# Recurrence of a two-layer hybrid block: adaLN loads asked for three places ahead, their products handed out at two points of a step

## The chip, the cores and the metric

One core of a Trainium2 chip. The metric is device time of one execution in microseconds. Times are in us unless marked otherwise. Engines: PE (matmuls; PEld is its weight load), DVE, ACT, POOL, and SP, which here only issues DMAs.

## The reference, cut to what matters

Two layers over 512 latent and 256 context tokens, width 1024. Each layer mixes with a gated linear recurrence (eight heads of 64, two directions) beside differential attention, then an MLP. Everything is modulated by six vectors of 1024 that one small product per layer makes from the conditioning vectors (adaLN):

```python
mod  = (sc  @ ada_w[l] + ada_b[l])[:, None, :]     # ada_w[l]: 1024 x 6144, fp32
modc =  scc @ ada_w[l] + ada_b[l]
sh1, s1, g1, sh2, s2, g2 = jnp.split(mod, 6, axis=-1)
...
def step(state, inp):                               # the recurrence, per token
    sa = jnp.einsum("bhvk,bhk->bhv", state, kk_t)
    state = state * w_t - sa * b_t + v_t * k_t
    y = jnp.einsum("bhvk,bhk->bhv", state, r_t)
...
o = jnp.concatenate([o_r, o_d], axis=-1) @ w_out[l]
x = x + g1 * rms_norm(o, g_post_mix[l])
f = sq_relu_mlp(modulate(rms_norm(x, g_pre_mlp[l]), sh2, s2), w_ff1[l], w_ff2[l])
x = x + g2 * rms_norm(f, g_post_mlp[l])
```

## The kernel before

The order of instructions on each engine is set when the program is built, by a scheduler that plays the program against a timeline of its own; each engine then runs its list strictly in order and waits at the head of it. Python code fixes the priorities: what is traced first goes first where both are ready.

A layer has three phases. `phase_wr` streams w_in, makes the recurrence's inputs and the attention, and ends with the recurrence (`rest`). `phase_o` multiplies by w_out, `phase_f` is the MLP. All weights come through one ring of three SBUF places of 512 KB (`raw`, tags raw0 to raw2), issued by SP: the w_in pieces, then the ada_w pieces of the recurrence, then the w_out pieces. A place is free again when the product or the split that reads it is done.

The recurrence has 12 steps a layer: six chunks of 128 tokens (`n`), two halves each (`j`), and in each step both directions (`d`) in turn. `step` yields behind each part: X of d = 0 and of d = 1 (PE lines 1186 and 1189, then ACT makes `xs` from it), `us` (L1198) and its copy `uv`, the state update (`us` again, L1210, then DVE's `sc` and ACT's `sbd`), and the output (L1226). That is eight yields; the last step has six (no state update), and in layer 2 the first four steps have six (no output). At each yield other work is handed out: `prep_b` of later chunks (L977 to L1054), the triangular inverses (`inv`, DVE lines 1100 and 1102, with relays through DRAM: `da`, `N`, `W`, `dn`, `dt`, `TT`, S<-dn; `merge` is L1152 to L1162 on PE) and the finish of completed token tiles (L1281 to L1295).

The adaLN product of the later vectors is such filler too. `ada_half` makes 512 columns of one vector from four pieces of ada_w; each piece is one `raw` load and eight small matmuls into `adar` (L265). Layer 1 needs 48 pieces (its own three kinds and the next layer's first), layer 2 needs 32. `ada` is a queue with credits: each step gives `ADA[l]` = 4 of them, all at the first yield, and the loads of that block are traced behind the step's own `uv` load on SP:

```python
for _ in step(n, j):
    work(1)
    if nst == 0:
        with tc.issue_after(self.gate.ins):
            ada(ADA[l])
    nst += 1
```

A product's load is traced just ahead of the product. `issue_after(x)` lets what a block traces on x's engine stand only behind x in that engine's list. In layer 1 the queue runs to the end of the last step; in layer 2 it is empty after the ninth.

Of the kernel before, what the change touches and what calls it, by code (L numbers as in the profile page):

```python
# [26 lines left out]
ADA = [4, 4]  # L27
# [137 lines left out]
class K:  # L165
# [16 lines left out]
    def run(self):  # L182
        with ExitStack() as es:
            self.cp = self.pool(es, "const", 1)
            self.sm = self.pool(es, "small", 6)
            self.rp = self.pool(es, "rowp", 1)
            self.rawp, self.raws, self.rawn = self.pool(es, "rawp", 1), 3, 0
            self.dr = es.enter_context(self.tc.tile_pool(name="dr", bufs=1, space=DRAM))
            self.setup()
            for l in range(L):  # L190
                self.layer(l)
                if self.stop is not None and self.stop.startswith(f"{l}"):
                    return
# [63 lines left out]
    def ada_half(self, l, ch, hf, ps, tag):  # L257

        nc = self.nc
        acc = ps.tile([128, 128], F32, name=self.n("adar"), tag=tag, bufs=1 if tag == "a" else 2)  # L260
        for kp in range(4):
            raw = self.raw(self.I["ada_w"][l, ch, hf, kp // 2][:, 2 * (kp % 2):2 * (kp % 2) + 2], [128, 2, 512])
            for k in range(2):
                for g in range(4):
                    nc.tensor.matmul(acc[32 * g:32 * g + 32, :], self.sc[:, 2 * kp + k, :],  # L265
                                     raw[:, k, g * 128:g * 128 + 128], start=(kp + k == 0), stop=(kp == 3 and k == 1),
                                     skip_group_check=True)
            if kp < 3:
                yield
        self.acc = acc  # L270

    def ada_cols(self, l, kind, ps, tag="m"):
# [653 lines left out]
    def recurrence(self, l, last, es, side):  # L926
# [240 lines left out]
        def step(n, j):  # L1167
            need_y = not (last and n < 2)
            final = n == 5 and j == 1
            mw = 128 if need_y else 64  # L1170
# [9 lines left out]
            for d in range(2):  # L1180
# [7 lines left out]
                for p in range(4):  # L1188
                    nc.tensor.matmul(X[0:mw, p * 128:p * 128 + 128], s["KR"][:, 2 * p + q, 0:mw], sbd[:, d, p, :],  # L1189
                                     start=False, stop=False, skip_group_check=True)  # L1190
# [3 lines left out]
            for d in range(2):  # L1194
                s = S[d]
                up = us[:, d]
                for h in range(8):
                    nc.tensor.matmul(up[(h % 2) * 64:(h % 2) * 64 + 64, h // 2, :], s["G"][:, h - h % 2 + s["q"], h % 2, 0:64],  # L1198
                                     s["xs"][:, h * 64:h * 64 + 64], start=True, stop=True, skip_group_check=True)
                for hf in range(2):  # L1200
                    nc.scalar.copy(s["uv"][0:64, hf:8:2, :], up[hf * 64:hf * 64 + 64])
                yield
            if not final:
                for d in range(2):
# [3 lines left out]
                    for h in range(8):  # L1208
                        hs = slice((h % 2) * 64, (h % 2) * 64 + 64)
                        nc.tensor.matmul(sp[hs, h // 2, :], s["BN"][:, h - h % 2 + q, hs], s["uv"][:, h, :],  # L1210
                                         start=True, stop=True, skip_group_check=True)
# [92 lines left out]
        def rest():  # L1304
# [16 lines left out]
            if l == 0:  # L1321
                ada.add(self.ada_cols(1, "mix", pa, "a"))
            work = Fill()
            prep_until(1)
            invs = Fill()
            for n in range(6):
# [3 lines left out]
                for j in range(2):  # L1330
                    nst = 0
                    for _ in step(n, j):
                        work(1)
                        if nst == 0:
                            with tc.issue_after(self.gate.ins):
                                ada(ADA[l])
                        nst += 1

                        for _ in range(4):
# [400 lines left out]
```

## Time and profile before

| | us |
|---|---|
| median of 3 runs | 2432.26 |
| the runs | 2419.16, 2433.48, 2432.26 |
| the profiled execution | 2426.55 |
| its span | 2424.8 |
| recurrence of layer 1, in the span | 490 to 757 |
| recurrence of layer 2 | 1756 to 2004 |

The span runs from the first to the last instruction; 1.75 us lie around it. The two recurrences are found by the products L1186 to L1226, which stand nowhere else. PEclk is the share of the full TensorE clock that was granted; 0.50 is 1.2 GHz and 1.00 is 2.4 GHz.

### The profile page before, as it was taken

What the parts mean: (1) busy time and instruction counts of PE and PEld (TensorE: products, weight loads), DVE (VectorE), ACT (ScalarE), POOL (GpSimd) and SP (SyncE); (2) the same over time, 40 slices, a digit from 0 to 9 for tenths busy, and PEclk for the clock granted to TensorE, in tenths of its full rate; (3) what the DMA queues carried; (4) which work ended last, traced back from release to release, by engine and by line L of the source; (5) the groups of instructions that cost most, each with busy time, mean ns of one, the idle gap of its engine ahead of it and who ended that gap; (6) DMA issues with size and microseconds to landing.
All of it is one profiled execution on the core that took longest, in us unless ns stands there. A gap on an engine that the chain in (4) does not pass through costs nothing.

```text
span 2424.8 us, 43738 instructions
## 1 busy us (share of the span) xinstructions
PE 2250.5 (93%) x17150; PEld 1903.9 (79%) x17150; DVE 1518.5 (63%) x2629; ACT 1174.4 (48%) x2393; POOL 803.6 (33%) x1048
## 2 busy tenths in 40 slices
PE   6999998899988999999999999999879988999997
PEld 5887887787777988888888887778767877788886
DVE  5456458647755675555556736665856575778784
ACT  4345547545534544333344435555735544555552
POOL 1212324832212343333330422323562121553530
PEclk9999999779998999999999999999879988999999
DMA  7543445377577521111112344454567664423230
GB/s 275 157 131 87 122 126 134 81 207 186 148 190 221 196 92 60 64 61 62 61 63 85 136 137 133 115 144 110 115 171 198 153 181 161 165 88 121 86 114 35
DMA packets 291630, 313.67 MB, mean 129 GB/s; under 512 B 139680, under 2 KB 220896, under 8 KB 291424
## 3 DMA queue, kind: packets, MB, share of 16 engines
q1 hardware_dynamic: 280320, 284.66, 38.8%
q0 software_dynamic: 10240, 23.08, 5.0%
q8 instruction: 135, 2.21, 0.4%
q10 hardware_dynamic: 864, 3.15, 0.3%
q14 instruction: 71, 0.58, 0.1%
HBM read 257.04 MB, written 53.77 MB: 128 GB/s over the span
## 4 chain that ended last, share of the span: by engine, by line
PE 66%; DVE 10%; DMA 8%; issue 5%; POOL 4%; ACT 4%; SPq 2%; ACTq 0%; POOLq 0%; DVEq 0%
PE pf L351 32%; PE pu L351 16%; PE po L351 4%; DMA raw<-in_ada_w 2%; PE po L832 2%; PE pb L1046 2%; PE sc L795 1%; DVE wl L1500 1%; POOL pr L1100 1%; POOL W L1102 1%; PE X L1189 1%; DVE nm L797 1%; PE X L1226 1%; PE adar L265 1%; PE ptr L815 1%
## 5 line engine op out<-in xcount | busy, mean ns | idle before, releaser
L1500 DVE TENSOR_TENSOR wl<-raw,wh 128x1024 fp32r<-128x1024 f32 x170 | 255.8, 1507 | 125.0 <-ACT wh L1499 124.2
L351 PE MATMUL pf<-hl,wh 128*128 128x512 f32 (+1 forms) x832 | 282.1, 342 | 0.0
L351 PE MATMUL pf<-hh,wh 128*128 128x512 f32 (+1 forms) x832 | 280.5, 342 | 0.6 <-ACT hh L397 0.6
L351 PE MATMUL pf<-hh,wl 128*128 128x512 f32 (+1 forms) x832 | 275.7, 342 | 0.0
L1499 ACT ACTIVATE wh<-raw 128x1024 fp32r<-128x1024 f32 x170 | 179.2, 1058 | 161.5 <-PE pf L351 143.9
L351 PE MATMUL pf<-wh,fah 128*128 128x512 f32 x570 | 224.5, 396 | 13.2 <-DVE fu L1633 7.2
L351 PE MATMUL pu<-hh,wh 128*128 128x512 f32 (+1 forms) x632 | 223.7, 354 | 4.8 <-DVE t L557 1.7
L351 PE MATMUL pf<-wl,fah 128*128 128x512 f32 x570 | 223.9, 394 | 0.7 <-DVE wl L1500 0.7
L351 PE MATMUL pf<-wh,fal 128*128 128x512 f32 x570 | 221.4, 394 | 1.8 <-DVE fal L1600 1.8
L351 PE MATMUL pu<-hh,wl 128*128 128x512 f32 (+1 forms) x632 | 218.6, 346 | 4.0 <-DVE wl L340 4.0
L351 PE MATMUL pu<-hl,wh 128*128 128x512 f32 (+1 forms) x632 | 218.0, 345 | 0.0
L797 DVE TENSOR_REDUCE nm<-sc 128x1 f32<-128x768 f32 (+1 forms) x160 | 132.5, 841 | 79.3 <-PE sc L795 78.5
L351 PEld LDWEIGHTS pf<-hl,wh 128*128 128x128 f32 x832 | 156.6, 188 | 20.0 <-DVE hl L399 0.2
L351 PEld LDWEIGHTS pf<-hh,wl 128*128 128x128 f32 x832 | 156.1, 188 | 20.0
L351 PEld LDWEIGHTS pf<-hh,wh 128*128 128x128 f32 x832 | 155.3, 188 | 20.4 <-ACT hh L397 0.8
L799 ACT ACTIVATE e<-sc,nm 128x768 f32<-128x768 f32 (+1 forms) x160 | 130.7, 821 | 53.9 <-DVE nm L797 44.3
L321 POOL TENSOR_TENSOR rs<-ms,pw 128x1 f32<-128x1 f32 (+2 forms) x60 | 56.7, 948 | 271.2 <-DVE ms L319 270.5
L351 PEld LDWEIGHTS pu<-hh,wh 128*128 128x128 f32 x632 | 121.2, 192 | 23.4 <-DVE t L557 2.4
L351 PEld LDWEIGHTS pf<-wh,fah 128*128 128x128 f32 x570 | 107.2, 188 | 40.6 <-ACT fah L1599 13.6
L1633 DVE TENSOR_TENSOR acc<-pf,acc 128x512 f32<-128x512 f32 x155 | 104.2, 682 | 53.9 <-PE pf L351 53.3
L351 PEld LDWEIGHTS pu<-hh,wl 128*128 128x128 f32 x632 | 121.0, 192 | 19.0 <-DVE wl L340 4.8
L351 PEld LDWEIGHTS pu<-hl,wh 128*128 128x128 f32 x632 | 121.1, 192 | 14.3 <-issue 1.7
(262 smaller groups left out, 5607.1 us busy)
## 6 DMA issues: line engine op xcount, KB each, us to landing
raw<-in_w_ff SPq DMA_DIRECT2D x128, 512.0 KB, 3.7
raw<-in_ada_w SPq DMA_DIRECT2D x96, 512.0 KB, 6.5
raw<-in_w_in SPq DMA_DIRECT2D x52, 512.0 KB, 4.0
ld<-zd SPq DMA_DIRECT2D x40, 384.0 KB, 5.5
ks<-qd POOLq DMA_DIRECT2D x64, 192.0 KB, 5.4
zd<-zr SPq DMA_DIRECT2D x22, 384.0 KB
raw<-in_w_out SPq DMA_DIRECT2D x16, 512.0 KB, 5.9
qs<-qd POOLq DMA_DIRECT2D x32, 192.0 KB, 5.9
```

The lines of the kernel that those rows point to most:

```text
L265: nc.tensor.matmul(acc[32 * g:32 * g + 32, :], self.sc[:, 2 * kp + k, :], raw[:, k, g * 128:g * 128 + 128], start=(kp + k == 0), stop=(kp ...
L321: nc.gpsimd.tensor_tensor(r, m, self.pw1.to_broadcast([128, cols]), ALU.pow)
L351: nc.tensor.matmul(out, a, b, start=(start and i == 0 and j == 0), stop=(i == n - 1 and j == 2), skip_group_check=not start)
L795: nc.tensor.matmul(sc[:, k0:k1], qs[:, br, tk], ks[:, br, k0:k1], start=True, stop=True)
L797: nc.vector.tensor_reduce(nm, sc, AX.X, ALU.max, negate=True)
L799: nc.scalar.activation(ee, sc, AF.Exp, bias=nm, accum_out=ls[:, br:br + 1])
L815: nc.tensor.transpose(pt[:, (k - k0) * 128:(k - k0) * 128 + 128], e[0][:, k * 128:k * 128 + 128], self.ident)
L832: nc.tensor.matmul(po, pT[:, k * 128:k * 128 + 128], vn[:, k, h * 64:h * 64 + 64], start=(k == 0), stop=(k == nk - 1))
L1046: nc.tensor.matmul(pgt[:, u, 0:nn], BK[hs, u, :], KR[hs, 2 * pp + u, 0:nn], start=True, stop=True, skip_group_check=True)
L1499: nc.scalar.activation(hi, src, AF.Copy)
L1500: nc.vector.tensor_tensor(lo, src, hi.bitcast(F32), sub)
L1633: nc.vector.tensor_tensor(d, p, d, add)
```

## The change

Loads and products are taken apart. `ada_todo` lists all pieces of a layer in the order of their products. Three loads are traced ahead of the first step, into the three places of the ring; then each product, once traced, asks for the piece three places on. `ada_half` takes the oldest load from `ada_ring`. The products are handed out at two points of a step, two credits each: at the second yield (behind X of d = 1) and at the sixth (behind the state update of d = 1; in steps of six yields the last one). `self.mark` is the last matmul traced by the step, and the block is traced behind it on PE as well as behind the `uv` load on SP.

```diff
+            self.ada_ring, self.ada_todo = [], iter(())
...
         for kp in range(4):
-            raw = self.raw(self.I["ada_w"][l, ch, hf, kp // 2][:, 2 * (kp % 2):2 * (kp % 2) + 2], [128, 2, 512])
+            raw = self.ada_ring.pop(0) if self.ada_ring else self.ada_load(l, ch, hf, kp)
...
+            self.ada_ahead(1)
             if kp < 3:
                 yield
         self.acc = acc
+
+    def ada_load(self, l, ch, hf, kp):
+        return self.raw(self.I["ada_w"][l, ch, hf, kp // 2][:, 2 * (kp % 2):2 * (kp % 2) + 2], [128, 2, 512])
+
+    def ada_ahead(self, n):
+        self.ada_ring.extend(self.ada_load(*p) for p in islice(self.ada_todo, n))
...
-                    nc.tensor.matmul(X[0:mw, p * 128:p * 128 + 128], s["KR"][:, 2 * p + q, 0:mw], sbd[:, d, p, :],
+                    self.mark = nc.tensor.matmul(X[0:mw, p * 128:p * 128 + 128], s["KR"][:, 2 * p + q, 0:mw], sbd[:, d, p, :],
...
+            self.ada_todo = ((m, ch, hf, kp) for m, chs in [(l, (2,)), (l, (3, 4)), (l, (5,))] + [(1, (0, 1))] * (1 - l)
+                             for hf in range(2) for ch in chs for kp in range(4))
+            self.ada_ahead(self.raws)
             work = Fill()
...
                     for _ in step(n, j):
                         work(1)
-                        if nst == 0:
-                            with tc.issue_after(self.gate.ins):
-                                ada(ADA[l])
                         nst += 1
+
+                        if nst in (2, 6):
+                            with tc.issue_after(self.gate.ins), tc.issue_after(self.mark.ins):
+                                ada(ADA[l] // 2)
```

The same `self.mark =` stands before the matmuls of `us` (L1198 of before) and of the state update (L1210). Lines below the first insertion move by one, those below `ada_load` by nine.

PE at the start of the third step of layer 1, before. `us` is the state update of the step ahead, X is this step's, `adar` the filler, `pb` the preparation of a later chunk.

```order
L1210 MATMUL us_5152<-uv_5680,S_3914 64x64 x8
L1186 MATMUL X_6081<-uv_5977,S_4371 128x64
L1186 MATMUL X_6081<-uv_5977,S_4371 64x64
L1189 MATMUL X_5979<-sbd_3609,S_4135 128x128 x4
L1186 MATMUL X_6081<-uv_5977,S_4371 64x64
L265 MATMUL adar_5995<-raw_6016,sc 32x128 x8
L1186 MATMUL X_6081<-uv_5977,S_4371 64x64 x3
L265 MATMUL adar_5995<-raw_6026,sc 32x128 x8
L1186 MATMUL X_6081<-uv_5977,S_4371 64x64 x2
L1046 MATMUL pb_6143<-S_3658,BK_6127 128x128
L1189 MATMUL X_6081<-sbd_3609,S_4371 128x128 x4
L1198 MATMUL us_5152<-xs_5130,S_4135 64x64 x8
```

The same place after:

```order
L1219 MATMUL us_5152<-uv_5686,S_3914 64x64 x8
L266 MATMUL adar_5730<-raw_5627,sc 32x128 x8
L266 MATMUL adar_5730<-raw_5739,sc 32x128 x8
L1198 MATMUL X_5985<-sbd_3609,S_4135 128x128 x4
L1195 MATMUL X_6042<-uv_5983,S_4371 64x64 x7
L1055 MATMUL pb_6127<-S_3658,BK_6111 128x128 x2
L1198 MATMUL X_6042<-sbd_3609,S_4371 128x128 x4
L266 MATMUL adar_6058<-raw_5749,sc 32x128 x8
L266 MATMUL adar_6058<-raw_5853,sc 32x128 x8
L1207 MATMUL us_5152<-xs_5130,S_4135 64x64 x8
```

The products stood between the parts of X; now two pairs stand behind `us` and behind X of d = 1.

PE at the end of layer 1's last step, before; `po` is the first product with w_out.

```order
L1198 MATMUL us_5152<-xs_5130,S_5374 64x64 x8
L1281 MATMUL pb_8675<-S_4371,cst 128x512
L1281 MATMUL pb_8709<-S_4371,cst 128x512
L265 MATMUL adar_8574<-raw_8725,sc 32x128 x8
L1226 MATMUL X_8545<-uv_8541,S_5374 64x64
L1198 MATMUL us_5152<-xs_5131,S_5501 64x64 x8
L1226 MATMUL X_8545<-uv_8541,S_5374 64x64 x7
L351 MATMUL po_8908<-wh_8780,hh_8770 128x256
```

And after:

```order
L266 MATMUL adar_8594<-raw_8517,sc 32x128 x8
L1235 MATMUL X_8551<-uv_8547,S_5331 64x64
L1207 MATMUL us_5152<-xs_5131,S_5482 64x64 x8
L1235 MATMUL X_8551<-uv_8547,S_5331 64x64 x7
L266 MATMUL adar_8594<-raw_8527,sc 32x128 x8
L1235 MATMUL X_8565<-uv_8549,S_5482 64x64 x8
L266 MATMUL adar_8594<-raw_8587,sc 32x128 x8
L266 MATMUL adar_8594<-raw_8603,sc 32x128 x8
L296 MATMUL adat_8737<-cst,row_8735 128x128
L360 MATMUL po_8908<-wh_8780,hh_8770 128x256
```

The last piece stood ahead of the last `us`; now the last three stand behind it. SP at the same place, before:

```order
L254 DMA raw_8595<-in_ada_w 128x1024
L1263 DMA S_4371<-zd_519 128x4x128
L1400 DMA ol_8838<-od_522 128x4x128
L1400 DMA ol_8850<-od_522 128x4x128
L1295 DMA od_522<-S_4371 128x4x128
L1263 DMA S_4371<-zd_519 128x4x128
L1264 DMA S_4371<-zd_519 128x4x128
L1400 DMA ol_8854<-od_522 128x4x128
L1295 DMA od_522<-S_4371 128x4x128
L1263 DMA S_4371<-zd_519 128x4x128
L254 DMA raw_8725<-in_ada_w 128x1024
L254 DMA raw_8826<-in_w_out 128x1024
```

And after:

```order
L255 DMA raw_8517<-in_ada_w 128x1024
L255 DMA raw_8527<-in_ada_w 128x1024
L1414 DMA ol_8858<-od_522 128x4x128
L1414 DMA ol_8862<-od_522 128x4x128
L1414 DMA ol_8874<-od_522 128x4x128
L255 DMA raw_8587<-in_ada_w 128x1024
L1293 DMA S_4371<-gd_520 128x4x128 x2
L255 DMA raw_8603<-in_ada_w 128x1024
L1414 DMA ol_8878<-od_522 128x4x128
L255 DMA raw_8826<-in_w_out 128x1024
```

The first w_out load stands three places behind the load of piece 46 (raw_8527) in the ring, and so behind that piece's product.

## Rows read from the trace of the kernel before

**Rows 1.** The page's chain that ended last, shares of the span by line.

```profile
PE pf L351 32%; PE pu L351 16%; PE po L351 4%; DMA raw<-in_ada_w 2%; PE po L832 2%; PE pb L1046 2%; PE sc L795 1%; DVE wl L1500 1%; POOL pr L1100 1%; POOL W L1102 1%; PE X L1189 1%; DVE nm L797 1%; PE X L1226 1%; PE adar L265 1%; PE ptr L815 1%
```

**Rows 2.** Stretches of the two recurrences: busy us by engine, PEclk, DMA share, GB/s.

```profile
490.00:757.00 267.00, 245.08 (x3463) 197.73 (x3462) 170.11 (x461) 129.22 (x305) 68.12 (x118) 0.87 0.76 197
1756.00:2004.00 248.00, 221.38 (x3206) 183.58 (x3208) 156.03 (x432) 120.46 (x281) 78.11 (x173) 0.86 0.69 178
```

**Rows 3.** PE's waits in 490 to 757: total us, times, longest.

```profile
PE adar L265 <- DMA raw<-in_ada_w: 13.6, 8, 2.8
```

**Rows 4.** PE's waits in 1756 to 2004.

```profile
PE pg L1152 <- DMA TT<-dt: 7.5, 5, 3.4
...
PE adar L265 <- DMA raw<-in_ada_w: 1.0, 2, 0.7
```

**Rows 5.** The chain inside 490 to 757, by line, shares of that stretch.

```profile
by line: DMA raw<-in_ada_w 16.9%; PE pb L1046 11.1%; PE adar L265 8.9%; PE X L1226 8.4%; PE X L1186 7.4%; PE X L1189 7.1%; PE us L1198 4.8%; PE pb L977 4.3%; PE us L1210 3.9%; DMA S<-gd 2.9%; PE pb L1053 2.6%; PE pb L1281 2.5%; DMA ol<-od 2
```

**Rows 6.** PE in 666 to 675.5 and 583 to 598, in order of time.

```profile
666.75 0.69 PE L1210 MATMUL us<-uv,S 128*64 128x64 f32 x16
...
669.90 1.16 PE L1189 MATMUL X<-sbd,S 128*128 128x128 f32 x8
...
674.41 0.65 PE L265 MATMUL adar<-raw,sc 128*32 128x128 f32 x16 [2.73 <-DMA raw<-in_ada_w]
...
583.36 0.69 PE L1210 MATMUL us<-uv,S 128*64 128x64 f32 x16
...
595.31 2.07 PE L1189 MATMUL X<-sbd,S 128*128 128x128 f32 x8
```

**Rows 7.** Loads of line 254 in 490 to 757.

```profile
DMA to landing us min/median/max: 3.7/5.6/8.8
```

**Rows 8.** Stretches at 0.50 of the clock in layer 1's recurrence, columns as in rows 2.

```profile
522.40:536.00 13.60, 13.60 (x214) 11.47 (x213) 2.35 (x6) 3.25 (x7) 0.00 (x0) 0.50 0.85 212
587.30:597.50 10.20, 9.62 (x56) 8.23 (x57) 5.46 (x16) 3.19 (x9) 3.99 (x5) 0.50 0.77 175
611.20:621.40 10.20, 10.20 (x65) 8.00 (x63) 5.42 (x13) 2.10 (x5) 4.02 (x3) 0.50 0.10 17
676.00:679.40 3.40, 3.40 (x45) 2.75 (x45) 1.54 (x7) 1.28 (x3) 0.00 (x0) 0.50 0.67 125
693.10:699.90 6.80, 5.86 (x74) 4.30 (x69) 2.15 (x9) 1.98 (x5) 0.00 (x0) 0.50 0.82 262
727.20:740.80 13.60, 9.78 (x95) 6.74 (x96) 8.34 (x11) 4.74 (x12) 6.04 (x4) 0.50 1.00 296
```

**Rows 9.** The chain in 470 to 810, in order of time: start, us, what.

```profile
565.14 1.09 PE X L1189 x8
...
588.94 2.01 PE X L1189 x8
...
661.90 1.01 PE adar L265 x32
```

**Rows 10.** SP's issues at layer 1's end, in order of time.

```profile
745.92 0.35 SPq L254 DMA_DIRECT2D raw<-in_w_out  x1
...
749.83 0.51 SPq L254 DMA_DIRECT2D raw<-in_w_out  x1
```

**Rows 11.** PE at the same place and where it next waits, in order of time.

```profile
756.23 0.69 PE L1198 MATMUL us<-xs,S 128*64 128x64 f32 x16
...
759.30 0.39 PE L351 MATMUL po<-wl,hh 128*128 128x256 f32 x1
...
787.54 0.38 PE L351 MATMUL po<-wh,hh 128*128 128x256 f32 x1 [1.23 <-ACT hh L1402]
```

**Rows 12.** ACT's split of the second w_out load.

```profile
755.69 1.06 ACT L339 ACTIVATE wh<-raw 128x1024 fp32r<-128x1024 f32 x1 [0.31 <-DMA raw<-in_w_out]
```

**Rows 13.** SP's own waits in 250 to 490, the phase ahead of layer 1's recurrence.

```profile
SPq L254 <- DVE wl L340: 12.4, 2, 11.3
```

**Rows 14.** DMA issues in 490 to 757: KB each, median us to landing.

```profile
N<-da SPq DMA_DIRECT2D x8, 256.0 KB, 8.3
```

More of the change, by code (lines that the diff above doesn't have):

```diff
@@ L1197, in step @@
                 for h in range(8):
-                    nc.tensor.matmul(up[(h % 2) * 64:(h % 2) * 64 + 64, h // 2, :], s["G"][:, h - h % 2 + s["q"], h % 2, 0:64],
+                    self.mark = nc.tensor.matmul(up[(h % 2) * 64:(h % 2) * 64 + 64, h // 2, :], s["G"][:, h - h % 2 + s["q"], h % 2, 0:64],
                                      s["xs"][:, h * 64:h * 64 + 64], start=True, stop=True, skip_group_check=True)
@@ L1209, in step @@
                         hs = slice((h % 2) * 64, (h % 2) * 64 + 64)
-                        nc.tensor.matmul(sp[hs, h // 2, :], s["BN"][:, h - h % 2 + q, hs], s["uv"][:, h, :],
+                        self.mark = nc.tensor.matmul(sp[hs, h // 2, :], s["BN"][:, h - h % 2 + q, hs], s["uv"][:, h, :],
                                          start=True, stop=True, skip_group_check=True)
```

## The prediction

> **What bounds the kernel now.** I read the page's chain first [rows 1]: two thirds of it are PE's products of the big phases, which the change leaves alone; loads of ada_w hold 2% of the span. So the question is the two recurrences, and I cut them out as stretches [rows 2]: 267 us in layer 1, 248 in layer 2, PE busy in 245.08 and 221.38 of them, DVE in 170 and 156, at a mean clock of 0.87 and 0.86. PE is the busiest engine in both. Then PE's own waits: in layer 1 it stood 13.6 us in front of adaLN products whose load had not landed, in eight waits [rows 3]; in layer 2 only 1.0 us, and there the relays of the inverse cost 7.5 us instead [rows 4]. The chain inside layer 1's recurrence names the same load with 16.9% [rows 5], which is 45 us. The reader is to see why 45 and 13.6 differ: the chain counts a load from its issue, while PE still had other products to do; only what is left when it has none is lost. The 13.6 us are what a load can give back directly, and only in layer 1.
>
> **The change, part by part.** All is set against the profiled execution, 2426.55, which lies 5.7 below the median; the sum is then laid on the median.
>
> *Loads three ahead.* The number of loads, products and bytes stays. A load is now asked for when the product three places on its left is done. With products in pairs at the second and the sixth yield, three loads of four have half a step or a whole one until their product. The fourth (asked behind the first product of the sixth yield, needed by the second product at the next step's second yield) has only the way from `us` of the state update to the end of X. In the trace that way took from 667.44 to 671.06, 3.6 us, at its shortest end, and from 584.05 to 597.38, 13.3, at a long one [rows 6]. A load lands in 5.6 us at the median [rows 7]. So the short ones still wait about 2.0 us, the long ones not. There are 11 such places in layer 1; I take three at the low end, 6 us left of 13.6: a gain of 7.6. Bounds: 13.6, if something stands between them each time, and a loss of 8.4, if all 11 wait 2.0.
>
> *The clock behind the waits.* Six stretches of layer 1's recurrence ran at 0.50 of the clock, 1.2 GHz [rows 8]. Ahead of the first five, within 6 us, PE stood before an adaLN product; the one at 676.0 begins behind the 2.73 us of [rows 6]. They sum to 44.2 us with PE busy in 42.7. The same eight products of X take 2.01 us there and 1.09 at full clock [rows 9], so 44.2 us are worth 24.0 at 2.4 GHz: 20.2 to be had. I take half, 10. The sixth stretch, at 727.2, has none so near, and layer 2, with 1.0 us of such waits, has no better a clock [rows 2, 4]: other waits bring the clock down as well, and some of them will come to light. Bounds 0 and 20.2. The Trainium skill ("TensorE: Matmul & The Clock Gate", section on HAM oscillation) charges time at the low clock that DMA waits cause at one half, all of it lost to the waits; by that the term would be an estimated 22, and the sum 12 us lower. The stretch at 727.2 and layer 2 speak against giving it all to this one wait.
>
> *Places on PE.* 32 adaLN products take 1.01 us [rows 9], so a pair of pieces is 0.5 us. They move from between the parts of X to behind it, beside ACT's `xs`, and behind `us`, beside DVE's and ACT's state update. That would be a cover if PE had nothing else there; it is busy in 245 of 267 us, so work moved is not work removed. I cost it at nothing; at best 24 half-steps of 0.5 are 12 us less ahead of X, at worst the same again behind `us`. What the block issues besides (per half vector a copy or two of a row on ACT or DVE, a transpose, and in the rows kind a load of 128 KB and two stores of 2 KB on SP) moves along with it, unchanged in number. The two fixed places are also where a late load now stops everything behind it on PE: X of the next step, or `us`.
>
> *The end of layer 1.* Here the change takes something away. Before, the first two w_out loads were issued at 745.92 and 749.83 [rows 10], while the last step was running, because the ring had places free. In the changed order the first w_out load waits for the product of piece 46, which stands behind the last `us` of the last step; that ended at 756.92 [rows 11], and with its 0.25 us the load goes out at about 757.3, the next behind another output product. From issue to split a load took 749.83 to 756.75, 6.9 us [rows 10, 12]. So the first `po`, at 759.30 before [rows 11], comes at about 764.3, 5 us late, and its second half a little later; I take 6. Late next is the finish of the last tiles, for which PE stood 1.23 us at 787.54 [rows 11]; that hides little. Bounds: 0, should SP's list let other work fill it, and 11, if the gap brings another stretch of 10.2 us at 0.50 (4.7 more at the ratio above). In layer 2 the queue is empty after nine of twelve steps, and its w_out loads are not touched.
>
> *Three loads ahead of the first step.* They go into SP's list in the phase before, where a load already made SP wait 11.3 us for a place [rows 13]; behind it now stand stores and loads of that phase. Its work on PE is matmuls on data that is there: cost 0, bounds 0 and 11.
>
> *Layer 2.* No waits to win. The fixed places may stop PE on a load as above; its steps wait for relays anyway. I take +2, bounds -5 (PE's list is smoother) and +10.
>
> Sum: -7.6 - 10 + 6 + 2 = -9.6. On the profiled execution 2416.9, on the median 2422.7, say 2423.
>
> **The rivals.** *A, all of it comes back:* the loads land in time throughout and the clock stays up: -13.6 - 20.2 + 6 = -27.8, 2404. For it: the five waits and their stretches are the only large holes in layer 1's PE. Against it: the short lead, and layer 2, which without such waits still takes 20.7 us a step (248 / 12).
>
> *B, small relays fall behind the big loads (slower):* SP feeds one queue. Layer 1's `N` loads, on which an inverse starts, took 8.3 us to land for half the bytes of an ada_w piece [rows 14]. If in each chunk one more piece of 512 KB stands ahead of them, at 197 GB/s [rows 2] that is 2.7 us; four inverses a layer whose merge the steps wait for, two layers: 21 us, with the end of layer 1 at its upper 11: +32, 2464, if no wait is won. It decides from where PE's waits at the merges (0 in layer 1 but for small ones, 7.5 in layer 2) grow by more than the adaLN waits shrink. Against it: the number of loads per step stays at four, and they come as two and two, where they came as three and one. The Trainium skill ("DMA: Bandwidth & Descriptors", section on queues, rings and completion order) has each DMA engine take descriptors in ring order, and a DMA issuer has one ring on each; by it a load asked for early is always paid by what is issued behind it. No row here shows how much of that reaches a step.
>
> *C, the wait only moves:* PE stops at the marks for as long as it did before, clock and all, and the end of layer 1 still costs 6 and layer 2 its 2: +8, 2440. For it: DMA moves 197 GB/s throughout, and a lead of 3.6 us is under the shortest landing, 3.7.
>
> That the change does not do what it says is excluded by the order: each load stands three products ahead.
>
> **How the numbers follow.** Forecast 0.45, A 0.22, B 0.13, C 0.20. About 1% (24 us) is what a measurement of this kernel can tell from no change: its three runs lie 14 us apart. Below 2408: most of A and a little of the forecast, 0.22. Above 2456.6: most of B and the upper end of C, 0.14. Range: from below A, 2398 (A without the 6 at the end), to where B begins in earnest, 2454.
>
> **What would show it.** Right: in layer 1's recurrence the wait of adaLN products for their loads falls from 13.6 to about 6, what is left sits at the products behind X, and the stretch's clock rises from 0.87 to above 0.90; behind the last step PE idles 5 us or more in front of `po`. Wrong: the wait is as long as before (C), it is gone and the clock too is at 0.95 (A), or waits at L1161 (the merge) and for `uv` grow (B). The sum is wrong as a whole if the built order, which also shifted preparation and relays a little, moves a stretch by more than these terms; layer 2, where nothing is to be won, would show that.

## Result, and the profile after

| | us |
|---|---|
| before, median of 4 runs | 2428.0 (2419.16 to 2433.48) |
| after, median of 4 runs | 2453.72 (2446.51 to 2459.71) |
| ratio after to before | 1.0106, 95% interval 1.0071 to 1.014 |
| profiled execution after | 2446.51, its span 2444.7 |

The change made the kernel about 1.1% slower, where the sum said 10 us faster. The profiled execution after is the fastest of its four, 7 us below their median, so the profiles show 20 of the 26 us.

First the span and the mean granted clock of the profiled execution after.

```profile
core 0: 2444.7 us, clock 0.938
```

Before it was 2424.8 us at 0.946. Time at half clock (1.2 GHz) is twice what is missing to 1: 2 x 0.054 x 2424.8 = 262 us before, 2 x 0.062 x 2444.7 = 303 us after. It is tempting to halve these 41 us, find 20.6, and put the whole difference of the spans, 19.9, down to the clock. But PE is idle in part of that time, and an idle us is no shorter at full clock. The pages' first lines part the two, before and then after.

```profile
PE 2250.5 (93%) x17150; PEld 1903.9 (79%) x17150; DVE 1518.5 (63%) x2629; ACT 1174.4 (48%) x2393; POOL 803.6 (33%) x1048
```

```profile
PE 2255.5 (92%) x17150; PEld 1915.6 (78%) x17150; DVE 1516.0 (62%) x2629; ACT 1171.9 (48%) x2393; POOL 800.7 (33%) x1048
```

PE was busy 5.0 us longer with the same number of products, and idle 14.9 us longer: 174.3 us before, 189.2 after.

The page's chain by line, after, beside [rows 1].

```profile
PE pf L360 32%; PE pu L360 15%; PE po L360 4%; PE po L841 2%; PE pb L1055 2%; PE sc L804 1%; DVE wl L1514 1%; PE X L1235 1%; DMA N<-da 1%; DMA TT<-dt 1%; PE X L1195 1%; PE pb L986 1%; PE adar L266 1%; DMA raw<-in_ada_w 1%; PE X L1198 1%
```

The adaLN load went from 2% to 1%, and two relays of the inverse, N<-da and TT<-dt, came up with 1% each. Now where the time stands, by the first product of each recurrence (X), the first and last product with w_out (`po`) of a layer, by their starts in us of the span:

| profiled execution | X, layer 1 | first po | last po | X, layer 2 | last po | span |
|---|---|---|---|---|---|---|
| before | 492.9 | 757.7 | 839.8 | 1756.7 | 2063.5 | 2424.8 |
| after | 495.8 | 762.7 | 840.6 | 1765.3 | 2083.4 | 2444.7 |

Layer 1 is even at its end (+0.8). From there to layer 2's last `po` it is 1223.7 us before and 1242.8 after: 19.1 us, nearly the whole loss of these two executions, lie in layer 2, some 8 of it ahead of the recurrence (in the attention) and some 11 from its first X on.

Stretches after, with columns as in [rows 2]: layer 1's recurrence with its end, then layer 2's recurrence.

```profile
495.00:764.00 269.00, 234.27 (x3486) 192.88 (x3484) 174.04 (x478) 131.00 (x309) 67.78 (x119) 0.90 0.74 193
1765.00:2028.00 263.00, 230.05 (x3227) 193.08 (x3227) 158.06 (x432) 121.67 (x286) 77.18 (x169) 0.82 0.65 161
```

In layer 1 the clock rose from 0.87 to 0.90, in layer 2 it fell from 0.86 to 0.82: 70 us at half clock became 95. From the first X of layer 2 to the recurrence's last product, 250.6 us before and 263.3 after, PE's busy time grew from 224.7 to 230.4 us and its idle time from 25.9 to 33.0. PE's waits in layer 1's recurrence after (total, times, longest):

```profile
PE adat L296 <- ACT row L293: 6.9, 2, 4.3
PE X L1235 <- ACT uv L1210: 5.6, 4, 3.0
PE pg L1161 <- DMA TT<-dt: 4.3, 3, 2.7
...
PE pb L1297 <- DVE Y L1285: 4.1, 2, 3.8
...
PE adar L266 <- DMA raw<-in_ada_w: 1.1, 1, 1.1
```

The 13.6 us of [rows 3] fell to 1.1. In their place stand waits that were not there or were small, four of them shown. PE's idle time did not fall: from the first X to the recurrence's last product it was 21.9 us of 266.5 before and 29.4 of 260.2 after. The stretch is shorter because PE's busy time fell, from 244.6 to 230.8 us. The same in layer 2: first two rows of before, to be read beside [rows 4], then the rows after.

```profile
PE us L1210 <- DVE st L1213: 8.5, 3, 5.2
PE X L1226 <- ACT uv L1201: 3.2, 3, 2.3
```

```profile
PE X L1235 <- ACT uv L1210: 8.0, 3, 4.8
PE pg L1161 <- DMA TT<-dt: 6.4, 4, 2.3
PE us L1219 <- DVE st L1222: 4.9, 1, 4.9
PE pb L986 <- DVE S L1057: 3.4, 3, 1.8
PE pb L1062 <- ACT ex L1031: 2.7, 1, 2.7
PE adar L266 <- DMA raw<-in_ada_w: 2.1, 3, 1.4
```

The waits for `uv` grew and two waits of the preparation (`pb`) are new; those at the merges and for `st` are shorter than before.

SP's own wait in layer 1 after, beside 13.6 us in ten waits for the same thing before:

```profile
SPq L255 <- PE adar L266: 37.6, 20, 5.8
```

SP now stands 24 us longer before loads whose place in the ring is still being read. Last, layer 1's end after, beside [rows 10, 11]: SP's issue of the first three w_out loads, then PE.

```profile
754.82 3.82 SPq L255 DMA_DIRECT2D raw<-in_w_out  x3
```

```profile
757.61 0.65 PE L266 MATMUL adar<-raw,sc 128*32 128x128 f32 x16 [1.06 <-DMA raw<-in_ada_w]
760.80 0.48 PE L296 MATMUL adat<-cst,row 128*128 128x128 f32 x1 [2.55 <-ACT row L293]
762.70 0.58 PE L360 MATMUL po<-wh,hh 128*128 128x256 f32 x1 [1.43 <-ACT wh L348]
```

The first w_out load goes nine us later than before, and PE stands three times before the first `po`.

### The profile page after: what moved, and what is told of

Read it like the earlier page. It is cut to its first block, busy times and chain, and to the rows that moved or that the text cites. A ratio compares the mean times of both kernels' runs of the same rounds, so it can differ in the third digit from the quotient of the medians.

```text
span 2444.7 us, 43775 instructions
## 1 busy us (share of the span) xinstructions
PE 2255.5 (92%) x17150; PEld 1915.6 (78%) x17150; DVE 1516.0 (62%) x2629; ACT 1171.9 (48%) x2393; POOL 800.7 (33%) x1048
## 4 chain that ended last, share of the span: by engine, by line
PE 67%; DVE 10%; DMA 9%; ACT 4%; issue 3%; POOL 3%; SPq 2%; ACTq 0%; POOLq 0%; DVEq 0%
PE pf L360 32%; PE pu L360 15%; PE po L360 4%; PE po L841 2%; PE pb L1055 2%; PE sc L804 1%; DVE wl L1514 1%; PE X L1235 1%; DMA N<-da 1%; DMA TT<-dt 1%; PE X L1195 1%; PE pb L986 1%; PE adar L266 1%; DMA raw<-in_ada_w 1%; PE X L1198 1%
## 5 line engine op out<-in xcount | busy, mean ns | idle before, releaser
L360 PE MATMUL pf<-wh,fah 128*128 128x512 f32 x570 | 226.0, 399 | 11.9 <-DVE fu L1647 7.2
L360 PEld LDWEIGHTS pf<-hh,wl 128*128 128x128 f32 x832 | 155.9, 188 | 19.9
L841 PEld LDWEIGHTS po<-vn,pT 128*128 128x128 f32 x832 | 116.6, 210 | 20.7 <-ACT pT L827 10.7
```

The lines of the kernel that those rows point to most:

```text
L360: nc.tensor.matmul(out, a, b, start=(start and i == 0 and j == 0), stop=(i == n - 1 and j == 2), skip_group_check=not start)
L841: nc.tensor.matmul(po, pT[:, k * 128:k * 128 + 128], vn[:, k, h * 64:h * 64 + 64], start=(k == 0), stop=(k == nk - 1))
```

## Experiments

Ratios are to the kernel before on the same chip, with 95% intervals. Each run was timed in five rounds; "layer 2" in a table is the time from layer 1's last `po` to layer 2's in its profile, against 1223.7 before. One profile of this can be off by some 15 us: the four kernels with layer 2 wholly in the order of before (`f1_l1new_l2order`, `p6_l1_rest_held`, `s2_l1_pool`, `g1_five`) show 0, -3, +9 and +15 there. Nor is a profiled execution always a typical one: that of `r3_l2_lead2` is the fastest of its twelve, 16 us below their median.

### Which layer, and which half of the change

`e1_l1only` and `e2_l2only` make the change in one layer; the other runs the code of before.

```diff
+            if l == 0:        # e2: l == 1
                 self.ada_todo = (...)
                 self.ada_ahead(self.raws)
...
-                        if nst in (2, 6):
+                        if l == 0 and nst in (2, 6):   # else: four credits at the first yield
```

> The change in layer 1 alone; layer 2 is written as before. Three theories for the 26 us that the change lost, of which the two traces put about 0 in layer 1, 8 ahead of layer 2's recurrence (attention) and 12 inside it. T1, layer 2's own loads and places cost it: this kernel takes the time of before within 5 us, and layer 2's recurrence takes 248 us. T2, the scheduler carries its timeline over from layer 1: the built order of layer 2 differs from before here too (DVE's list in the attention is the one of the whole change), so the 8 us ahead of layer 2's recurrence are lost here as well, +8, and the recurrence may go anywhere in 248 to 260. T3, layer 1's end eats its gain and nothing else matters: the recurrence of layer 1 is 8 us shorter, the first output product comes no earlier.

> The change in layer 2 alone; layer 1 is as before to the instruction, and so is DVE's list in layer 2's attention but for 4 rows. T1, layer 2's own loads and places cost: +12 to +20, most of the loss. T2, the order carried over from layer 1 costs: the attention is as before (recurrence of layer 2 starts at 1756 to 1759), and inside the recurrence 0 to +12.

`e3_ring_only` keeps the loads ahead and puts the products back to the first yield; `e4_place_only` drops `ada_todo`, so that each load is traced just ahead of its product.

```diff
-                        if nst in (2, 6):               # e3
+                        if nst == 0: ... ada(ADA[l])
-            self.ada_todo = (...)                       # e4
-            self.ada_ahead(self.raws)
```

> Loads three products ahead in both layers, products as before at the first yield only, behind the uv load. If the fixed places on PE cost the time, this one keeps the gain of layer 1 (recurrence 8 to 10 us shorter than 255.7) without the loss in layer 2: -10 to 0. If the early loads cost (three ahead of the first step, and small relays behind them), it is as slow as the whole change: +20 to +26.

> Products at the two places behind the marks in both layers, each load traced just ahead of its product as before. If the places cost the time: +20 or more, with the load waits of layer 1 still there (13.6 us or more, since nothing stands between). If the early loads cost: at most +8, and layer 2 within 5 us of before. What the loads' lead alone is worth is the difference of this kernel to the whole change: 8 us in layer 1 by the traces.

| run | median | ratio | layer 2 |
|---|---|---|---|
| e1_l1only | 2441.97 | 1.0067 (1.0036 to 1.0099) | +12.6 |
| e2_l2only | 2451.55 | 1.0097 (1.0064 to 1.0129) | +23.3 |
| e3_ring_only | 2466.31 | 1.0145 (1.0098 to 1.0193) | +8.4 |
| e4_place_only | 2457.08 | 1.0103 (1.006 to 1.0146) | +28.3 |

All four are slower, none brings the gain of layer 1 home, and no half is innocent; `e3_ring_only` came in at +35 us, beyond both of its forecasts, and still waits 12.6 us for loads in layer 1. `e1_l1only` loses its time in layer 2, where its code is that of before. What differs there is the built order: the scheduler carries its timeline over from layer 1, and in layer 2 the lists of PE and DVE differ from those of before in hundreds of instructions. So the order had to be taken out of the comparison.

### The order of layer 2 by itself

`hold_order` gives the scheduler, for each engine, edges of issue order from each instruction to the one ahead of it in a table (no waits).

```diff
+    for e, moves in table.items():
+        seq = [mine[e][k + m] for k, m in enumerate(moves)]
+        for a, b in zip(seq, seq[1:]):
+            tc.add_manual_dep(b, a.name, <NoSync>, reason="order")
...
         K(tc, I, out).run()
+        hold_order(tc, nc, first)      # first: where layer 2 begins
```

`f1_l1new_l2order` is `e1_l1only` with layer 2 in the order of before; `f2_l2order_of_e1` is the code of before with layer 2 in the order of `e1_l1only`; `g1_five` is `f1_l1new_l2order` with `ada(3 if nst == 1 else 2)` in place of two and two.

> Layer 1 as the change has it, layer 2's code as before, and layer 2's instructions held on every engine in the order that they have in the kernel before (edges of issue order alone, no waits). It differs from the run with the change in layer 1 alone (2442 against 2431) only in that order. If the order that the scheduler gave layer 2 costs the 11 us: within 5 us of before, 2426 to 2436, and layer 2's recurrence at 248 to 253 us with about 68 us at half clock. If something that layer 1 leaves behind costs it (transfers, the clock's state): 2442 again, recurrence 259.

> The counterpart: the code of before throughout and layer 1 as before, but layer 2 held in the order that it has where layer 1 is changed. No load and no product is moved by hand anywhere. If the order costs: +8 to +14, 2439 to 2445, recurrence of layer 2 at 257 to 262 with some 95 us at half clock. If not: 2431.

`n1_kinds` is a neutral change to the kernel before:

```diff
+            if l == 0:
+                kinds = (kinds[1], kinds[0], kinds[2])
```

> A neutral change to the kernel before: in layer 1 the first two kinds of adaLN vectors change places in the queue; the same loads, products and places of credits. The scheduler's order changes in layer 1's recurrence and again in layer 2. If any new order of layer 2 tends to be worse than that of before: +5 to +20, lost in layer 2 and to the clock. If the loads' lead and the two places are the cause: within 5 us of before.

> Layer 1 as changed but with five credits a step (three at the second yield, two at the sixth), so that the products end two steps earlier and the w_out loads are free to go before the last step's end; layer 2 in the order of before. If the end of layer 1 is what ate the 8 us of its recurrence: -5 to -10 against before (2421 to 2426), the first output product at 750 to 754 instead of 757.7. If more products early only move the waits: 2431 or slower.

| run | median | ratio | layer 2 |
|---|---|---|---|
| f1_l1new_l2order | 2427.58 | 0.998 (0.9958 to 1.0002) | +0.1 |
| f2_l2order_of_e1 | 2443.53 | 1.0053 (1.0027 to 1.0078) | +10.1 |
| n1_kinds | 2444.02 | 1.0039 (1.0009 to 1.0068) | +25.7 |
| g1_five | 2457.76 | 1.0094 (1.0067 to 1.0121) | +15.1 |

The order alone costs 0.5% where no instruction was added or moved by hand (`f2_l2order_of_e1`). Its recurrence of layer 2, columns as in [rows 2]:

```profile
1764.00:2017.00 253.00, 229.45 (x3237) 191.65 (x3237) 156.77 (x433) 121.75 (x286) 75.77 (x169) 0.83 0.67 170
```

It shows the lower clock, 0.83, though the recurrence takes 252.5 us where 257 to 262 were expected; the rest of its +10.1 lies ahead of it. From layer 1's last `po` to layer 2's first X it takes 926 us, much as after the change (925), against 917 before. But that difference is no sign of the order: `g1_five` and `s2_l1_pool`, with layer 2 in the order of before, take 927 there. Whether the 8 us ahead of layer 2's recurrence belong to the change, to the order or to the scatter is not shown. `g1_five` missed its forecast: five credits a step brought the first `po` to 740.7, but its last to 855.0, 15 us late. My expectation had looked only at the beginning.

### The change with the rest of the order held

Is the order, then, the cause? `p3_l2_rest_held`, `p6_l1_rest_held` and `p5_all_rest_held` make the change in layer 2, layer 1 and both, and hold all but the adaLN work (its loads, products, row copies, transposes; in layer 1 also the first w_out splits) in the order of before: the table of `hold_order` leaves out `adar`, `adat`, `row`, `growd`, `modA`, `modB` and the loads of ada_w. The adaLN work goes where the scheduler puts it behind its marks.

> The change in layer 2 alone, cleanly: layer 1 as before, and in layer 2 everything but the adaLN work (its loads, products, row copies, transposes) held in the order of before. The run with the change in layer 2 and an order of the scheduler's own was 1.0097 of before. If the new order of everything else is what costs: within 6 us of before, 2426 to 2438. If the loads ahead and the two places cost of themselves: +10 to +20.

> The change in layer 1 alone, cleanly: everything but layer 1's adaLN work and the first splits of w_out held in the order of before; layer 2 is wholly that of before. By the terms of the prediction for layer 1 (-7.6 for the waits, -10 for the clock behind them, +6 at the end): -12 against before. If the waits only move: 0 to +6. The run with the scheduler's own order of layer 1 and layer 2 held was 0.998.

> The whole change in both layers, with everything but the adaLN work held in the order of before. If the order of the rest made the loss: the sum of the two runs beside it, by the prediction -10 and at most +5. If the change costs by itself: +15 or more, as the change as built (+26).

| run | median | ratio | layer 2 |
|---|---|---|---|
| p3_l2_rest_held | 2451.23 | 1.0069 (1.0046 to 1.0093) | +26.6 |
| p6_l1_rest_held | 2442.15 | 1.0024 (0.9994 to 1.0054) | -2.5 |
| p5_all_rest_held | 2463.64 | 1.0109 (1.0078 to 1.0141) | +24.3 |

Not alone: with the order held the whole change costs 1.09%, as built 1.06%. The two layers (0.24 and 0.69) add up to that within the intervals. A new order of layer 2 alone costs as much, though (`e1_l1only` against `f1_l1new_l2order`, 0.9%), so in the kernel as built the shares of the two are not parted. In `p6_l1_rest_held` PE still waits for loads in layer 1's recurrence:

```profile
PE adar L267 <- DMA raw<-in_ada_w: 12.9, 5, 5.7
```

13.6 before, 12.9 here: fewer and longer waits, and the clean change wins nothing in layer 1. Why the loads still come late in that order was not looked into. Layer 2's recurrence in `p3_l2_rest_held`, and PE's first wait in it:

```profile
1754.40:2032.60 278.20, 236.89 (x3250) 199.55 (x3249) 158.03 (x435) 122.41 (x286) 77.21 (x170) 0.79 0.62 153
```

```profile
PE pg L1162 <- DMA TT<-dt: 15.1, 5, 3.8
```

The wait for the relays at the merges doubled from the 7.5 of [rows 4], and that of X for `sbd` rose from 1.5 to 6.1. The clock is at 0.79: 117 us at half clock against 70. Of the 27.6 us by which this stretch is longer than before (278.2 against 250.6), 15.4 are idle time of PE (41.3 against 25.9); its busy time grew by 12.2, from 224.7 to 236.9, with the same products.

### Filling the waits to keep the clock up

`w1_warm_l2` is `f1_l1new_l2order` with products that nobody reads, put into PE's waits of layer 2's recurrence, all other instructions in the same order.

```diff
+    def warm(self, out, k, start):
+        for _ in range(k):
+            self.nc.tensor.matmul(out, w[:, 0:64], self.cst[:, 0:512], start=start, stop=start, ...)
```

> The kernel with layer 1 changed and layer 2 held in the order of before (0.998 of before), with 17 products of 128x512 whose results nobody reads put into the places in layer 2's recurrence where its trace shows PE waiting, each wait followed by a stretch at half clock: 1 ahead of the first X, 3, 1 and 2 ahead of merges 0, 1 and 2, 5 and 3 ahead of two state updates, 2 ahead of an output. By the rows they are 0.87 us each, 14.8 us in gaps of some 17. If the half clock comes from these waits: the 61 us at half clock in that recurrence fall below 30, and the time falls by 10 to 25 us against that kernel, to 2403 to 2418. If not, nothing is won, and what doesn't fit into the waits is lost: 0 to +10.

It came to 2438.2, 1.0013 (0.9991 to 1.0034), against 0.998 of the kernel it was made from. Layer 2's recurrence in `f1_l1new_l2order` and then in `w1_warm_l2`:

```profile
1752.20:2003.10 250.90, 220.90 (x3249) 182.70 (x3249) 157.67 (x435) 122.52 (x286) 79.22 (x173) 0.88 0.70 175
```

```profile
1761.50:2017.10 255.60, 233.43 (x3284) 182.83 (x3283) 158.27 (x435) 123.11 (x286) 77.36 (x170) 0.91 0.67 170
```

The clock rose from 0.88 to 0.91 (60 us at half clock to 46), PE was busy 12.5 us longer, and the time didn't fall. My expectation of 10 to 25 us failed: the time at half clock fell as the waits were filled, but the work put into them cost at least what the clock gave back. The two kernels' executions also lie 8 us apart at layer 1's end, where their orders are the same; that much is scatter.

### Loads or places, and by which way

In layer 2 alone, order held: `r1_l2_loads` moves only SP's adaLN loads, `r2_l2_places` the products to their two points, each with its load just ahead of it, and `r3_l2_lead2` is `p3_l2_rest_held` with a lead of two.

```diff
-                        if nst in (2, 6):       # r1: products as before
-            self.ada_todo = (...)               # r2: each load ahead of its product
-            self.ada_ahead(self.raws)           # r3:
+            self.ada_ahead(2)
```

> Layer 2's loads alone: layer 1 as before, the products of layer 2 where they were, every engine held in the order of before but for SP's adaLN loads of layer 2, which are asked for three products ahead. The clean change in layer 2 (loads and places, the rest held) was 1.0069 of before, with SP standing 35.6 us before loads whose place was not free, against 16 to 19, and PE 15.1 us at the merges, against 7.5 to 9.3. If the early loads cost it, by holding SP and with it the small relays behind them: +10 to +17, merges' wait above 12. If the places on PE cost it: within 5 of before.

> Layer 2's places alone: products in pairs at the two points, each load traced just ahead of its product, everything but the adaLN work held in the order of before. If the places cost it: +10 to +17 with PE waiting on loads or at the merges; if the loads: within 5 of before, at most +8 for loads that come late.

> As the clean change in layer 2, but each load is asked for two products ahead of its own instead of three, so that its place in the ring was left by the product before the last one and SP need not stand for it. If SP's waits for places are the mechanism: SP's wait before adaLN loads falls from 35.6 to below 15, the merges' wait from 15 to below 11, and the time comes back to within 7 us of before. If not: 1.006 to 1.008 again.

`s1_l2_pool` and `s2_l1_pool` are `p3_l2_rest_held` and `f1_l1new_l2order` with the changed layer's adaLN loads issued by `nc.gpsimd` in place of `nc.sync`. In `s2_l1_pool` layer 1 is not held: some 950 of PE's products stand elsewhere there than in `f1_l1new_l2order`, so it does not show the issuer's effect alone.

> The clean change in layer 2 (1.0069 of before), but its adaLN loads are issued by POOL, so that no load that has no free place can stand in SP's list ahead of the relays of the inverses and of the uv loads. A lead of two did not test this: SP stood 31.8 us before the loads as against 35.6. If SP's standing is the mechanism: the merges' wait on PE falls from 15 to below 10 us, and the time comes back to within 7 us of before (ratio below 1.003). If the loads cost by the transfers themselves, or the places by their own: 1.005 to 1.008. POOL then stands before the loads instead, and what waits for POOL (S, sg of the preparation) may be late: bounded by the 77 us of 250 that it is busy, at most +10.

> Layer 1 as changed with its loads issued by POOL, layer 2 held in the order of before; with SP's loads it was 0.998 of before, and SP stood 37.6 us before loads without a place. If SP's standing costs layer 1 as well: 0.992 to 0.997. If not, 0.998 to 1.003.

`r4_l2_loads_cut` is `r1_l2_loads` with a quarter of each load:

```diff
-        return self.raw(src, [128, 2, 512])
+        return self.raw(src[:, :, 0:128] if l == 1 and ch > 1 else src, [128, 2, 512])
```

> As the run with layer 2's loads alone moved ahead (1.0042 of before, PE 14.4 us at the merges, SP 28.9 us before loads without a place), but in layer 2 each of these loads brings only the first 128 of its 512 columns, and the products use these four times over; three quarters of that product's weights are left out. The lists of all engines stay as they were but for two places on SP. If the relays of the inverses are late because 512 KB stand ahead of them in the transfers: the merges' wait falls below 9 us and the time to within 4 us of before or under it (below 1.001). If they are late because SP stands in front of a load whose place isn't free: that wait stays near 29 us, the merges' near 14, and the ratio at 1.003 to 1.006.

| run | median | ratio | layer 2 |
|---|---|---|---|
| r1_l2_loads | 2447.35 | 1.0042 (1.0016 to 1.0068) | +15.4 |
| r2_l2_places | 2449.01 | 1.0055 (1.003 to 1.0081) | +28.4 |
| r3_l2_lead2 | 2452.72 | 1.0064 (1.004 to 1.0087) | +11.9 |
| s1_l2_pool | 2451.57 | 1.0088 (1.0061 to 1.0115) | +25.8 |
| s2_l1_pool | 2452.41 | 1.0087 (1.0064 to 1.0109) | +8.5 |
| r4_l2_loads_cut | 2430.68 | 0.9988 (0.996 to 1.0016) | -4.6 |

Either half costs by itself, and both together cost little more than one. At the merges' first products (`pg` of `TT`) PE waited 5.7 to 9.3 us in the five kernels whose layer 2 is that of before (`before`, `f1_l1new_l2order`, `g1_five`, `p6_l1_rest_held`, `s2_l1_pool`), and 12.3 to 20.8 in the five with the order held and early loads of 512 KB in layer 2 (`p3_l2_rest_held`, `p5_all_rest_held`, `r1_l2_loads`, `r3_l2_lead2`, `s1_l2_pool`). The two ranges do not meet. `r3_l2_lead2` told nothing of the mechanism: SP stood 31.8 us before loads as against 35.6. In `s1_l2_pool` SP no longer stands before them (it stands 18.0 us before two late w_out loads), yet PE waits longer at the merges, and POOL stands instead; PE's first wait in layer 2's recurrence, then POOL's:

```profile
PE pg L1163 <- DMA TT<-dt: 20.8, 5, 6.6
```

```profile
POOL raw L256 <- PE adar L267: 24.1, 13, 10.2
```

So the relays can be late without SP standing before the adaLN loads; since POOL's standing comes into it, the run doesn't clear SP either. In `s2_l1_pool` POOL stood 93.7 us, PE waited 25.2 at layer 1's merges, and layer 1's last `po` came 24 us late. The clearest pair is `r1_l2_loads` and `r4_l2_loads_cut`, whose lists differ in two places on SP. PE's wait at the merges, first with 512 KB a load, then with 128 KB:

```profile
PE pg L1162 <- DMA TT<-dt: 14.4, 5, 5.5
```

```profile
PE pg L1163 <- DMA TT<-dt: 6.5, 5, 3.5
```

The second of layer 2's merges shows the loads at work, because both kernels have two of them directly ahead of the relay. SP's issues and then PE, with 512 KB:

```profile
1816.05 0.85 SPq L256 DMA_DIRECT2D raw<-in_ada_w  x2
...
1817.49 2.38 SPq L1142 DMA_DIRECT2D TT<-dt  x2
```

```profile
1824.17 0.31 PE L1162 MATMUL pg<-TT,S 32*32 32x32 f32 x2 [4.19 <-DMA TT<-dt]
```

and with 128 KB:

```profile
1823.12 0.92 SPq L256 DMA_DIRECT2D raw<-in_ada_w  x2
...
1824.65 2.03 SPq L1143 DMA_DIRECT2D TT<-dt  x2
```

```profile
1828.48 0.31 PE L1163 MATMUL pg<-TT,S 32*32 32x32 f32 x2 [1.49 <-DMA TT<-dt]
```

From the relay's issue to PE's product it takes 6.7 us behind two loads of 512 KB and 3.8 behind two of 128 KB; in the kernel before, with no load between the two relays, 3.3. With a quarter of the bytes the merges wait as little as before, and the loss is gone. So the bytes of the early loads are needed for it, and one way in which they act is seen: through the relay issued right behind them. It is not shown to be the only one: SP's wait before the loads fell as well, from 28.9 to 18.5 us, where my expectation had it stay, and no run cut the bytes in the order of before, so what fewer bytes give by themselves is not known.

For the places (`r2_l2_places`) no such pair was run, and SP's wait before the loads rose there too, from 16.1 to 32.7 us. The wait at the merges is 5.9 us, so it loses in another way: of the 24.5 us by which its recurrence is longer than before (275.1 against 250.6) only 6.2 are idle time (32.1 against 25.9), and 18.3 are busy time, at a clock of 0.78. What brings the clock down there stays open.

## Why the prediction was wrong

By the sum layer 1 was to end 11.6 us earlier (-7.6 - 10 + 6) and layer 2 to lose 2. In the profiles layer 1 ended even (+0.8) and layer 2 lost 19.1. So the larger part of the miss is layer 2's term, and the rest is layer 1's gain, which was spent again before the layer's end.

**Loads three ahead (-7.6).** As built the wait for loads fell further than I said, to 1.1 us, and from the first product of X to the last (L1186) layer 1 took 247.8 us in place of 255.8. But over the whole recurrence PE's idle time grew, from 21.9 to 29.4 us: other waits took more than the place of the one that went. With the rest held the wait for loads stayed at 12.9 us and nothing was won. A good part of the 13.6 therefore went with the new order, which brought the waits for `row`, `uv`, TT and Y. I had counted only the wait that goes.

**The clock behind the waits (-10).** From 0.87 of 267 us to 0.90 of 269: 69 us at half clock to 54, worth at most some 8. The size is near the term, but the cause that I gave is not shown: in `p6_l1_rest_held` the waits for loads stayed at 12.9 us and the clock stood at 0.89 all the same, and in `e2_l2only`, whose layer 1 is that of before, at 0.88. That the number came near is luck. The Trainium skill ("TensorE: Matmul & The Clock Gate", section on HAM oscillation) counts half of the time at the low clock that DMA waits cause as lost, which would have given the estimated 22. That is not borne out here as a gain: 54 us at half clock were left with the load waits gone, as the stretch at 727.2 had warned.

**Places on PE (0).** Wrong in layer 2. `r2_l2_places` puts them, with the loads that move along, at +0.55% in layer 2 alone, about 13 us. "Work moved is not work removed" was no reason for nothing. For layer 1 no run parts the places from the order.

**The end of layer 1 (+6).** Right in kind, short in size: the last X ended 5.1 us earlier and the first `po` came 5.0 later, +10 together, near my upper bound of 11. I had also read the first `po` of before at 759.30; the trace has one at 757.7 already. The loads went out about when I said; ACT's split and its copy of `row` came on top. The products with w_out then made up some 4 us.

**Three early loads (0).** Mis-sized. In the seven kernels whose layer 1 has them on SP and the products at two points, the first X stands at 493.6 to 498.6, at the mean 495.9; in the ten that have neither there, at 488.1 to 492.9, mean 490.9; in `e4_place_only`, which has only the places, at 489.6. So they cost some 5 us, inside the bounds of 0 and 11. In `e3_ring_only`, which has them and the products at the first yield, the first X stands at 507.6, beyond the bound; how much of that is its order is not known.

**Layer 2 (+2, bounds -5 to +10).** This is the step that failed. It measured +19 as built, and +0.69% (17 us) with the order held. I reasoned that there was no wait to win, so little could happen, and priced only a stop of PE at the marks; that a load asked for earlier delays the relays issued behind it I had only in B, and I gave the places nothing. With the order held, the early loads doubled PE's wait at the merges (7.5 to 15.1 us) and the stretch lost 15.4 us to idle time and 12.2 to longer busy time at a clock of 0.79. As built the picture is another: the merges wait no longer than before, and the recurrence grew by 12.7 us, 7.1 of them idle time (the waits for `uv` and in the preparation) and 5.7 busy time. How much of that is the new order, which alone costs 0.5% (`f2_l2order_of_e1`), stays open.

**The rivals.** B, at 0.13, named the mechanism that the five kernels with early loads and `r4_l2_loads_cut` show in layer 2. That its 21 us are near what layer 2 lost is luck: they were for both layers, its 8.3 us for `N` [rows 14] are the one landing that the trace tells of eight, and layer 1's merges waited only 4.3 us after the change. By the sign I gave for it (merges' waits growing by more than the adaLN waits shrink) the built kernel would not have shown it: there the merges of layer 2 wait 6.4 us, 7.5 before. On the Trainium skill's page that the prediction names there ("DMA: Bandwidth & Descriptors", section on queues, rings and completion order), each DMA engine takes descriptors in ring order. The trace agrees where two loads stand directly ahead of a relay, 6.7 us behind 512 KB each and 3.8 behind 128 KB; but in `s1_l2_pool`, where the loads are issued by POOL and go by queue q0 in place of SP's q1, the merges wait longest, 20.8 us, so there something other than the order in one ring delays them. C (the wait only moves) is what `p6_l1_rest_held` shows for layer 1. A fell.

**My warning** that a shifted order could outweigh the terms was right in that an order is worth 0.4 to 0.9% (`f2_l2order_of_e1`, `n1_kinds`, `e1_l1only` against `f1_l1new_l2order`), and it had no price in the sum. It is not needed for the loss: held, the change loses the same. No run of the whole work beat the kernel before by more than it can be told; the nearest is the change in layer 1 alone with layer 2's order held, 0.998 (0.9958 to 1.0002).

## What to carry to other kernels

Before loads are asked for earlier, find the small transfers that a serial chain waits for and price their delay in every stage where the loads move, above all where the loads had been in time: there the change can only cost. When a scheduler sets the order, an edit in one stage reorders the next; hold the rest of the order to see what the edit itself does. Watch an engine's whole idle time, not the one wait that you remove: in layer 1 that wait went from 13.6 to 1.1 us and PE's idle time still grew by 7.5. And do not put time at half clock down to the clock alone: part of it is idle.

## What the runs showed of the hardware

With an order held, some waits come back to a tenth: PE's three waits for `uv` in layer 2's output products were 3.2 us, the longest 2.3, in the kernel before, in `f1_l1new_l2order` and in `p3_l2_rest_held`; others do not (at the merges 7.5, 9.3 and 15.1 us). In one pair of like places, two loads of 512 KB issued 1.4 us ahead of a relay of 64 KB kept PE waiting for it 6.7 us from its issue, and two of 128 KB 3.8 us. And the kernel before itself ran between 2412.9 and 2444.4 us in the twenty runs beside the first experiments, at mean clocks of 0.937 to 0.953: its own scatter is as wide as the loss.
